# First modulation in four steps of 256 channels, idle matmuls during the input loads, tiles 4 to 7 in buffers of their own, sines at a fixed place

## Chip, cores and metric

The kernel runs on one core of a Trainium2 chip. The metric is device time in microseconds: the median of the runs shown. A core has TensorE (PE, the matrix engine, with weight loads shown apart as PEld), VectorE (DVE), ScalarE (ACT), GpSimd (POOL) and SyncE (SP, which here only issues DMAs). Each engine works through a queue of its own in order; semaphores tie the queues together.

## What is computed

Two layers of a hybrid decoder block over 1024 tokens of width 1024, all in fp32. The part that matters here is the head of a layer:

```python
mod = c_act @ w_mod + b_mod
shift, scale, gate = jnp.split(mod[:, None, :], 3, axis=-1)
h = rms_norm(x, pre_gain) * (1.0 + scale) + shift
proj = h @ w_in
(aq, ak, av, ag, rq, rk, rv, rg, gq, gk, gv, gg, ga) = jnp.split(proj, IN_SPLITS, axis=-1)
```

`c_act = silu(c)` is one vector of 1024. Three groups of heads follow (windowed attention and retention with rotary angles from `positions`, and gated linear attention), then gates, an output projection and `x + gate * rms_norm(y)`.

## The kernel before

A token tile is 128 tokens; tiles 0 to 3 are handled by `first_stage`, tiles 4 to 7 by jobs that run behind it. A projection is done with fp32r operands split in a high and a low part (`hi`, `lo`), three passes: hi by hi, hi by lo, lo by hi. `hT[(0, p)]` holds the transposed, modulated input of two tiles, in both parts. `gg`, `rg`, `rq`, `rk` are blocks of 256 columns of `w_in`; `gg` carries 16 extra columns for the gate logits, hence 272. A block is loaded in four DMAs into `st` buffers (five of them) and converted by ACT (high part, L495) and POOL or DVE (low part, L499).

What `first_stage` does (L674 to L804), in its order:

- Loads: ACT issues the identity, the positions, the bias rows (L679, L680), the frequencies of the rotary tables (`freq`) and `w_ga`. SP issues the four x tiles, then the first layer's shift and scale weights `wm` (8 MB, eight blocks of 128 channels, two DMAs each, L694) with the four `gg` loads between them, then the four `rg` loads.
- `tables` (L360) computes the rotary angles on DVE: about 15 operations of 128x512, which the caller takes one at a time with `more(n)`. Near its end ACT computes two sines (L385, L386), each with a table of its own function to be loaded; tanh is in another table.
- For each x tile: the sum of squares on ACT (L727), one step on DVE (L604), a power on POOL (L607), the scaling on DVE (L732).
- Eight steps, one per block `b` of 128 channels. `turn(b)` transposes the four tiles' block into two PSUM tiles `at` (pool `mm`, three banks) and multiplies `c_act` by `wm` into `pm`: eight matmuls of 256 columns, four at a time in column groups. Then ACT copies the row out (L761), two matmuls with the vector `sel` bring it into columns ("selections"), DVE makes `gain` and `shift` (L767, L769), and the transposed tiles are scaled and shifted: tiles 0 and 1 on ACT (L777, high part L778), tiles 2 and 3 on DVE (L774, L775), the low parts on DVE (L779). `products(b - 1, ...)` multiplies the block before by `gg`, 12 matmuls of 272 columns in the accumulators `acc[0..3]`; they stand around the selections, so that PE has work while the others make the columns.

After that the four `rg` conversions, the products of the last block, and the loads of tiles 4 to 7: into the two halves of a buffer of tag `mx` (L794), into `kT0`, and into two `t2` buffers (L798). These buffers held x tiles 0 to 3 before. Then the projection of `rg` begins (79 matmuls of 256 columns in a row), in which the jobs for tiles 4 to 7 are mixed: squares on ACT (L621), scaling on DVE (L637), for each tile two groups of four transposes (L187, pool `aux`, five banks), read by ACT (L651) and DVE (L653), conversions L657 and L658.

Outside `first_stage` a planner with a clock of its own (`clk`, the costs in the table `L`) decides where in PE's order a job's matmuls stand; the other engines' order is then set by a scheduler. Inside it the order is that of the code. The end of the sines and the transposes of their table are such a job (`table_job`).

Of the kernel before, what the change touches and what calls it, by code (L numbers as in the profile page):

```python
# [17 lines left out]
P = 128  # L18
# [75 lines left out]
def trunk(ctx: ExitStack, tc: tile.TileContext, ins, cst, out):  # L94
# [579 lines left out]
    def first_stage():  # L674
        for j in range(2):
            mod_tile(0, j)
        shift, gain = modc[(0, 0)], modc[(0, 1)]
        rows = t1()[0:24, 0:P]
# [4 lines left out]
        freq = cload("freq", eng=A)  # L683
# [5 lines left out]
        wm = bp.tile([P, 4 * SLOT], F32, tag="arena1", name="wm").rearrange("p (b k n) -> p b k n", b=KT, k=KT)  # L689
        gg, rg = load(0, "gg", "AG"), load(0, "rg", "AV")  # L690
        gg.issue()
        def wm_load(b):
            for i in range(2):
                nc.sync.dma_start(wm[:, b, 4 * i:4 * i + 4], w_m0[b, :, 4 * i:4 * i + 4].rearrange("p k j n -> p k (j n)"))  # L694

        for b in range(KT - 1):
            wm_load(b)
            if b in (1, 3, 4):
                gg.issue()
# [9 lines left out]
        pposf = aux()  # L709
        transp(pposf[:, 0:8], posr, ident[0:8, 0:8])  # L710
        V.tensor_copy(posf, pposf[:, 0:8])
        more(1)
# [3 lines left out]
        more(2)  # L716
        pr = aux()
        transp(pr[:, 0:24], rows, ident[0:24, 0:24])
        rc = small(24)
        V.tensor_copy(rc, pr[:, 0:24])  # L720
        base = small(8)
        V.tensor_scalar(base, rc[:, 8:16], 1.0, None, ALU.add)
        sel = small(1)
        V.tensor_reduce(sel, ident[:, 0:97:32], AX.X, ALU.add)
        for t in range(4):
            ss = small(1)
            A.activation(wm[:, KT - 1, 4 * (t % 2):4 * (t % 2) + 4].rearrange("p k n -> p (k n)"), xe[t], AF.Square, accum_out=ss)  # L727
            r = rstd_of(ss, 1, 1.0 / D, EPS)
            if t == 3:
                A.activation(w[:, 0, :, 256:272], low, AF.Copy)  # L730
                V.tensor_tensor(w[:, 1, :, 256:272], low, f(w[:, 0, :, 256:272]), ALU.subtract)
            V.tensor_scalar(xe[t], xe[t], r, None, ALU.mult)  # L732
        gg.convert()
        wm_load(KT - 1)
        for _ in range(4):
            rg.issue()
        acc = [aux() for _ in range(4)]
        pm = aux()
# [3 lines left out]
        def products(b, ts):  # L742
            for t in ts:
                h = hT[(0, t // 2)]
                c = slice((t % 2) * P, (t % 2) * P + P)
                for i, (x, y) in enumerate(((0, 0), (0, 1), (1, 0))):
                    mult(acc[t][:, 0:272], h[:, x, b, c], w[:, y, b, 0:272], b == 0 and i == 0, b == KT - 1 and i == 2)

        def turn(b):
# [9 lines left out]
        for b in range(KT):  # L759
            row = t1()  # L760
            A.activation(row, pm[:, 0:256], AF.Copy)  # L761
            if b:
                products(b - 1, (0,))
            c0 = 256 + 2 * b
            for j in range(2):
                mult(pm[:, c0 + j:c0 + j + 1], row[:, j * P:(j + 1) * P], sel, True, True)
            V.scalar_tensor_tensor(gain[:, b:b + 1], pm[:, c0 + 1:c0 + 2], base[:, b:b + 1], rc[:, 16 + b:17 + b],  # L767
                                   ALU.add, ALU.mult)
            V.tensor_tensor(shift[:, b:b + 1], pm[:, c0:c0 + 1], rc[:, b:b + 1], ALU.add)  # L769
            for p in range(2):  # L770
                hf = t1()
                hi, lo = (hT[(0, p)][:, a, b, 0:256] for a in range(2))
                if p:
                    V.tensor_scalar(hf, at[p][:, 0:256], gain[:, b:b + 1], shift[:, b:b + 1], ALU.mult, ALU.add)  # L774
                    V.tensor_copy(hi, hf)  # L775
                else:
                    A.activation(hf, at[p][:, 0:256], AF.Identity, scale=gain[:, b:b + 1], bias=shift[:, b:b + 1])  # L777
                    A.activation(hi, hf, AF.Copy)  # L778
                V.tensor_tensor(lo, hf, f(hi), ALU.subtract)  # L779
            if b:  # L780
                products(b - 1, (1, 2, 3))
            if b < KT - 1:
                at = turn(b + 1)
            if b in (0, 2, 4):
                gg.convert()
            if b < 6:
# [4 lines left out]
        products(KT - 1, range(4))  # L791
        x6 = gp.tile([P, D], F32, tag="kT0", name=nm("xk"), bufs=1)
        for t, xt in zip(range(4, NT), x_pair() + [x6]):
            nc.sync.dma_start(xt, x_in[0, t * P:(t + 1) * P, :])  # L794
            late.append([xt[:, 512 * j:512 * j + 512] for j in range(2)])
        late.append([t2(), t2()])
        for j in range(2):
            nc.sync.dma_start(late[3][j], x_in[0, 7 * P:8 * P, 512 * j:512 * j + 512])  # L798
# [4 lines left out]
        late.append(sin)  # L803
# [41 lines left out]

# [970 lines left out]
```

## Time and profile before

| | us |
|---|---|
| median of 3 runs | 994.59 (992.64 to 995.18) |
| profiled execution | 999.38 |
| its span, first to last instruction | 997.7 |
| PE busy in it | 963.3 (97%) |
| granted PE clock, mean | 0.992 |

A row of the timeline has start, duration, engine, line, operation, out<-in with the shape, and the number of instructions merged; in brackets the idle time ahead of it and what ended that. `SPq` and `ACTq` are the queues that issue DMAs. In a row of the windows `(x25)` is a number of instructions, and the number behind the five engines is the granted PE clock as a share of full speed. One fp32 matmul shows as two matmul records.

### The profile page before, as it was taken

Reading aid. Unit: us, or ns where it says so; the run is one execution under the profiler, and the core shown is the slowest. Engines: PE = TensorE matmul, PEld = TensorE weight load, DVE = VectorE, ACT = ScalarE, POOL = GpSimd, SP = SyncE. Lnnn points to the kernel's source line nnn. Section 1 sums busy time; section 2 is a strip of 40 time slices with the busy share of each in tenths; the row PEclk is TensorE's granted clock in tenths of the full one; section 3 lists DMA queues with packets and bytes.
Section 4 is the critical chain, followed back from the end, with each engine's and each line's share of the span. In section 5 each row is a group of like instructions: output and inputs, shape, how many; then the busy total and the mean of one; then the engine's idle time right before and its main releaser. Section 6 shows DMA issues by size and latency. Waiting matters only on the chain. (4 is left out here: it accounts for less than half of the span.)

```text
span 997.7 us, 19627 instructions
## 1 busy us (share of the span) xinstructions
PE 963.3 (97%) x7188; PEld 826.3 (83%) x7188; DVE 681.6 (68%) x1622; ACT 400.8 (40%) x1127; POOL 246.6 (25%) x310
## 2 busy tenths in 40 slices
PE   3979999999999999999999999999999999999996
PEld 1779999989997777777879999998999877777775
DVE  3668667867666787665598176785766577676876
ACT  3387210333322565633356232133332256664231
POOL 2132101233220233430115010123322033544000
PEclk9998999999999999999999999999999999999998
DMA  9456713433225355577656131242122324388783
GB/s 344 170 163 182 206 60 106 152 109 104 93 91 185 90 148 160 179 230 250 216 202 210 48 107 33 93 151 85 50 97 86 127 76 134 112 271 262 247 274 125
DMA packets 109457, 150.35 MB, mean 151 GB/s; under 512 B 12168, under 2 KB 59820, under 8 KB 109360
## 3 DMA queue, kind: packets, MB, share of 16 engines
q1 hardware_dynamic: 97920, 134.75, 43.0%
q10 hardware_dynamic: 11440, 14.34, 3.9%
q8 instruction: 57, 0.93, 0.4%
q14 instruction: 40, 0.33, 0.1%
HBM read 110.25 MB, written 36.70 MB: 147 GB/s over the span
## 5 line engine op out<-in xcount | busy, mean ns | idle before, releaser
L172 PE MATMUL mm<-arena,arena 128*128 128x256 f32 (+2 forms) x1824 | 300.5, 318 | 0.5 <-DVE t L1233 0.4
L172 PE MATMUL mm<-arena 128*128 128x256 f32 (+2 forms) x1728 | 284.9, 318 | 0.0
L172 PEld LDWEIGHTS mm<-arena,arena 128*128 128x128 f32 x1824 | 255.3, 191 | 26.0 <-issue 4.8
L172 PEld LDWEIGHTS mm<-arena 128*128 128x128 f32 x1728 | 240.4, 189 | 24.3 <-issue 4.2
L172 PE MATMUL mm<-arena,mx 128*128 128x512 f32 (+1 forms) x564 | 130.9, 388 | 0.5 <-DVE t L1434 0.5
L607 POOL TENSOR_TENSOR sm<-sm,mhalf 128x1 f32<-128x1 f32 (+1 forms) x64 | 56.8, 888 | 297.5 <-DVE sm L604 162.5
L172 PEld LDWEIGHTS mm<-arena,mx 128*128 128x128 f32 x564 | 101.5, 188 | 24.6 <-issue 1.5
L156 ACT ACTIVATE t<-aux 128x256 f32<-128x256 f32 (+2 forms) x124 | 52.3, 437 | 93.5 <-PE aux L187 80.0
L156 ACT ACTIVATE arena<-st 128x512 fp32r<-128x512 f32 x94 | 56.1, 628 | 48.3 <-DMA st<-in_w_in_dram 17.1
L499 POOL TENSOR_TENSOR arena<-st,arena 128x512 fp32r<-128x512 f32 x31 | 45.0, 1451 | 116.1 <-ACT arena L156 74.9
L991 POOL TENSOR_TENSOR smx<-smx,sm 128x512 f32<-128x512 f32 x32 | 35.0, 1094 | 134.2 <-DVE sm L990 113.2
L987 ACT ACTIVATE smx<-smx,sm 128x129 f32<-128x129 f32 x128 | 49.9, 393 | 32.7 <-DVE sm L984 32.6
L499 DVE TENSOR_TENSOR arena<-st,arena 128x512 fp32r<-128x512 f32 x77 | 59.9, 799 | 4.1 <-ACT arena L156 2.4
L318 DVE SCALAR_TENSOR_TENSOR acc<-ms,c_act,acc 128x512 f32<-128x512 f32 x60 | 45.1, 751 | 15.3 <-DMA ms<-in_w_mod_dram 14.7
L1035 ACT ACTIVATE t<-aux 128x256 f32<-128x256 f32 x32 | 12.3, 384 | 77.5 <-PE aux L172 71.3
L172 PEld LDWEIGHTS aux<-t,mx 32*128 32x128 f32 (+1 forms) x896 | 39.8, 187 | 3.9 <-issue 1.7
L172 PE MATMUL aux<-t,mx 32*128 32x32 f32 (+1 forms) x896 | 40.9, 272 | 0.0
L187 PE MATMUL aux<-c_ident,t 128*128 128x128 f32 (+2 forms) x187 | 33.2, 277 | 5.2 <-DMA t<-in_pre_norm_gain_dram 3.3
L1337 DVE SCALAR_TENSOR_TENSOR t<-t,sm,t 128x512 f32<-128x512 f32 x32 | 23.3, 752 | 20.2 <-DMA t<-in_x_dram 13.5
L982 DVE COPY_PREDICATED smx<-c_curmask,aux 128x256 f32<-128x256 int32 x64 | 25.3, 446 | 16.4 <-ACT smx L156 14.6
L172 PEld LDWEIGHTS aux<-kT,mx 64*128 64x128 f32 x384 | 24.7, 185 | 11.8 <-issue 5.2
L1040 DVE TENSOR_TENSOR t<-aux,sm 128x256 f32<-128x256 f32 x32 | 13.6, 425 | 27.3 <-POOL sm L607 27.3
(252 smaller groups left out, 1435.1 us busy)
## 6 DMA issues: line engine op xcount, KB each, us to landing
st<-in_w_in_dram SPq DMA_DIRECT2D x96, 256.0 KB, 4.0
ms<-in_w_mod_dram SPq DMA_DIRECT2D x64, 256.0 KB, 3.7
mx<-mixS SPq DMA_DIRECT2D x20, 512.0 KB, 5.2
st<-in_w_last_dram SPq DMA_DIRECT2D x36, 256.0 KB, 3.7
wm<-in_w_m_dram SPq DMA_DIRECT2D x16, 512.0 KB, 9.7
mixS<-t SPq DMA_DIRECT2D x40, 128.0 KB, 1.9
t<-in_x_dram SPq DMA_DIRECT2D x18, 256.0 KB, 6.1
mixS<-t ACTq DMA_DIRECT2D x32, 128.0 KB, 3.1
```

Of the source, the lines that this page charges most:

```text
L156: A.activation(dst, src, AF.Copy)
L172: T.matmul(dst, lhsT, rhs, start=start, stop=stop)
L187: T.transpose(dst, src, idn)
L318: V.scalar_tensor_tensor(acc, wt, c_act[:, k:k + 1], acc, ALU.mult, ALU.add)
L499: e.tensor_tensor(lo, st, f(hi), ALU.subtract)
L607: G.tensor_tensor(r, r, mhalf[:, :w], ALU.pow)
L982: V.copy_predicated(sv, curmask.unsqueeze(1).to_broadcast((P, 2, P)), pv[:, :, n // P - 1, :])
L987: A.activation(sm[:, h, :], sm[:, h, :], AF.Exp, bias=mx[:, h:h + 1], accum_out=sums[:, h:h + 1])
L991: eng("pn").tensor_tensor(sm[:, :, 0:128], sm[:, :, 0:128], rs.unsqueeze(2).to_broadcast((P, 4, P)), ALU.mult)
L1035: A.activation(sq, po, AF.Square)
L1040: V.tensor_tensor(h4(g1), h4(po), r.unsqueeze(2).to_broadcast((P, 4, 64)), ALU.mult)
L1337: V.scalar_tensor_tensor(xt[j], yg[j], r, xt[j], ALU.mult, ALU.add)
```

## The change

- `wm` is cut in four steps of 256 channels. A step does eight transposes, eight matmuls of 512 columns into all of `pm`, four selections, and scales and shifts both of its blocks: the first on ACT, the second on DVE, each for all four tiles at once (512 columns). The selections write to a bank `pc` of the pool `mm`, which it keeps for the whole stage. The products of a step (24 matmuls) follow one step later; for step 1 three tiles of them stand ahead of the selections, otherwise one; after the last step they run pass by pass over all tiles.
- `spin(n)` multiplies the identity by itself into an accumulator that is overwritten later: 6 times after the transpose of the positions, 18 times after that of the bias rows, 6 times in step 1.
- The frequencies are loaded ahead of the bias rows. All angle operations on DVE now have fixed places (three ahead of the tiles, one with each of tiles 0 to 2, eight after step 0's `turn`), the two sines stand after step 0 on ACT, one table load for both, and a tanh of no use to the result after step 2 brings tanh's table back. `table_job` is gone; the table's transposes are a job of their own, due after 16.0 instead of the old delays.
- Tiles 4 to 7 are loaded in halves into three `smx` buffers, three of the modulation's buffers (`ms`) and the two `t2` buffers.

```diff
-        for b in range(KT - 1):
-            wm_load(b)
-            if b in (1, 3, 4):
-                gg.issue()
+        for s in range(3):
+            gg.issue()
+            wm_load(s)
+        acc = [aux() for _ in range(4)]
+        pm = aux()
+        def spin(n):
+            for _ in range(n):
+                mult(acc[3][:, 0:P], ident, ident, True, True)
...
         def turn(b):
-            for t in range(4):
-                transp(at[t // 2][:, t % 2 * P:t % 2 * P + P], xe[t][:, b * P:b * P + P], ident)
+            for i in range(2):
+                for t in range(4):
+                    transp(at[i][:, t * P:t * P + P], xe[t][:, (2 * s + i) * P:(2 * s + i + 1) * P], ident)
+            if s == 1:
+                spin(6)
             for k in range(KT):
                 g = k % 4
-                mult(pm[32 * g:32 * g + 32, 0:256], c_act[:, k:k + 1].to_broadcast((P, 32)), wm[:, b, k], k < 4, k > 3, 0.11)
+                mult(pm[32 * g:32 * g + 32, :], c_act[:, k:k + 1].to_broadcast((P, 32)), wm[:, s, k], k < 4, k > 3, 0.22)
...
         at = turn(0)
-        for b in range(KT):
+        more(8)
+        for s in range(4):
+            row = t2()
+            A.activation(row, pm, AF.Copy)
+            n = 3 if s == 1 else 1
+            if s:
+                products(s - 1, range(n))
+            for i in range(4):
+                mult(pc[:, 4 * s + i:4 * s + i + 1], row[:, i * P:(i + 1) * P], sel, True, True)
...
+            if s < 3:
+                at = turn(s + 1)
+                gg.convert()
+            if s == 0:
+                more(1)
+            elif s == 1:
+                more(2)
+            elif s == 2:
+                A.activation(th0, c_nat, AF.Tanh, scale=0.5)
...
-        x6 = gp.tile([P, D], F32, tag="kT0", name=nm("xk"), bufs=1)
-        for t, xt in zip(range(4, NT), x_pair() + [x6]):
-            nc.sync.dma_start(xt, x_in[0, t * P:(t + 1) * P, :])
+        kept = [gp.tile([P, 528], F32, tag="smx", name=nm("xl"), bufs=SMB)[:, 0:512] for _ in range(3)]
+        kept += [mod_stage() for _ in range(3)] + [t2(), t2()]
+        for t in range(4, NT):
+            xt = kept[2 * t - 8:2 * t - 6]
+            for j in range(2):
+                nc.sync.dma_start(xt[j], x_in[0, t * P:(t + 1) * P, 512 * j:512 * j + 512])
```

PE's order at the start of the program, before (`c_ident` is the identity, `xk` and `mx` are x tiles 0, 1 and 2, 3, `arena` holds weights and `hT`):

```order
L187 MATMUL aux_137<-c_ident,posr 128x8
L187 MATMUL aux_147<-c_ident,t_6_98 128x24
L187 MATMUL mm_198<-c_ident,xk_105 128x128
L187 MATMUL mm_198<-c_ident,xk_106 128x128
L187 MATMUL mm_199<-c_ident,mx_107 128x128 x2
L172 MATMUL aux_197<-wm,c_act 32x256 x8
L172 MATMUL aux_197<-sm_153,t_40_212 128x1 x2
```

and now:

```order
L187 MATMUL mm_132<-c_ident,posr 128x8
L172 MATMUL aux_128<-c_ident 128x128 x6
L187 MATMUL mm_148<-c_ident,t_6_100 128x24
L172 MATMUL aux_128<-c_ident 128x128 x18
L187 MATMUL mm_218<-c_ident,xk_105 128x128
L187 MATMUL mm_218<-c_ident,xk_106 128x128
L187 MATMUL mm_218<-c_ident,mx_107 128x128 x2
L187 MATMUL mm_219<-c_ident,xk_105 128x128
L187 MATMUL mm_219<-c_ident,xk_106 128x128
L187 MATMUL mm_219<-c_ident,mx_107 128x128 x2
L172 MATMUL aux_129<-wm,c_act 32x512 x8
L172 MATMUL mm_217<-sm_170,t_41_244 128x1 x4
```

Twenty-four idle matmuls stand ahead of the first tile, and a step has twice the transposes and selections.

ACT's order from the last block's scaling (L777) to the squares of tile 4 (L621), before (`sm` and `t` are small tiles and tiles of 256 or 512 columns):

```order
L777 ACTIVATE t_76_501<-mm_478,mod_4_96,mod_5_97 128x256
L385 ACT_TABLE_LOAD
L385 ACTIVATE sincos<-mx_140 128x8x64
L778 ACTIVATE arena_71<-t_76_501 128x256
L495 ACTIVATE arena_518<-st_185 128x512
L495 ACTIVATE arena_518<-st_187 128x512
L495 ACTIVATE arena_518<-st_189 128x512
L495 ACTIVATE arena_518<-st_191 128x512
L1060 ACTIVATE sm_586<-aux_193 128x16
L1052 ACT_TABLE_LOAD
L1052 ACTIVATE t_86_591<-aux_193 128x256
L1060 ACTIVATE sm_596<-aux_194 128x16
```

and now, from the last step's scaling (L802):

```order
L802 ACTIVATE t_61_433<-mm_396,mod_4_96,mod_5_97 128x512
L803 ACTIVATE arena_71<-t_61_433 128x2x256
L495 ACTIVATE arena_459<-st_209 128x512
L495 ACTIVATE arena_459<-st_211 128x512
L495 ACTIVATE arena_459<-st_213 128x512
L495 ACTIVATE arena_459<-st_215 128x512
L1087 ACTIVATE sm_546<-aux_125 128x16
L1079 ACTIVATE t_75_551<-aux_125 128x256
L1087 ACTIVATE sm_556<-aux_126 128x16
L1079 ACTIVATE t_79_561<-aux_126 128x256
```

The sine and the table loads are gone from this place; the second sine (L386), which stood a few rows further with two more table loads around it, is gone from there too.

SP's order behind the last gg load, before (`st` are weight blocks):

```order
L694 DMA wm<-in_w_m_dram 128x1024 x6
L161 DMA st_185<-in_w_in_dram 128x512
L161 DMA st_187<-in_w_in_dram 128x512
L161 DMA st_189<-in_w_in_dram 128x512
L161 DMA st_191<-in_w_in_dram 128x512
L794 DMA mx_540<-in_x_dram 128x1024 x2
L794 DMA xk_539<-in_x_dram 128x1024
L798 DMA t_80_544<-in_x_dram 128x512
L798 DMA t_81_545<-in_x_dram 128x512
```

and now:

```order
L694 DMA wm<-in_w_m_dram 128x2048 x2
L161 DMA st_209<-in_w_in_dram 128x512
L161 DMA st_211<-in_w_in_dram 128x512
L161 DMA st_213<-in_w_in_dram 128x512
L161 DMA st_215<-in_w_in_dram 128x512
L831 DMA xl_492<-in_x_dram 128x512
L831 DMA xl_493<-in_x_dram 128x512
L831 DMA xl_494<-in_x_dram 128x512
L831 DMA ms_495<-in_x_dram 128x512
```

The place in the queue is the same; the buffers written are others, and each tile comes in two halves.

More of the change, by code (lines that the diff above doesn't have):

```diff
@@ L733, in first_stage, with product, products @@
         gg.convert()
-        wm_load(KT - 1)
+        gg.issue()
+        wm_load(3)
         for _ in range(4):
             rg.issue()
-        acc = [aux() for _ in range(4)]
-        pm = aux()
         for p in range(2):
             hT[(0, p)] = place(TOK[0][p])
-        def products(b, ts):
+        def product(t, b, x, y, start, stop):
+            h = hT[(0, t // 2)]
+            mult(acc[t][:, 0:272], h[:, x, b, (t % 2) * P:(t % 2) * P + P], w[:, y, b, 0:272], start, stop)
+        def products(s, ts):
@@ L802, in first_stage @@
             flag(("hT", 0, t))
-        late.append(sin)
         return acc
@@ L1757, in trunk @@
     job(gla_log(0, 0))
-    job(table_job(late[4]))
+    job(tables_T())
     job(late_consts())
```

112 lines of the change are left out of this document (54 added, 58 removed).

## Prediction

> **What bounds the kernel now.** I read the page's busy times first, then busy time by stage, then by shorter stretches for the granted clock, then the timeline of the stages that have holes.
>
> ```profile
> span 997.7 us, 19627 instructions
> ...
> PE 963.3 (97%) x7188; PEld 826.3 (83%) x7188; DVE 681.6 (68%) x1622; ACT 400.8 (40%) x1127; POOL 246.6 (25%) x310
> ```
>
> TensorE (PE) is busy 97% of the span, so 34.4 us of holes are all that any change to waits can win, plus what PE loses while its clock is granted at half. The busy times by stage (columns: length, busy time of PE, weight loads, DVE, ACT, POOL, granted clock, DMA share, GB/s) show where the holes are:
>
> ```profile
> 0.00:30.00 30.00, 13.83 (x74) 8.51 (x78) 12.65 (x34) 10.06 (x19) 6.38 (x16) 1.00 0.94 354
> 52.78:58.33 5.55, 2.81 (x13) 2.22 (x13) 3.57 (x8) 5.52 (x9) 1.17 (x1) 0.91 0.90 305
> 71.70:100.00 28.30, 25.20 (x187) 24.84 (x185) 23.27 (x58) 21.13 (x52) 6.86 (x9) 0.88 0.63 186
> 100.00:980.00 880.00, 875.52 (x6558) 752.40 (x6557) 607.64 (x1438) 341.98 (x992) 219.90 (x264) 1.00 0.46 144
> ```
>
> From 100 to 980 us PE has 4.5 us of holes; before 100 us it has 16.2 + 2.7 + 3.1 = 22 us, all where the change works. A hole costs twice, as the next table shows, cut at multiples of 3.41 us:
>
> ```profile
> 23.17:26.59 3.42, 3.42 (x25) 2.38 (x18) 2.52 (x6) 0.38 (x1) 1.11 (x1) 1.00 1.03 395
> 26.59:30.00 3.41, 3.41 (x21) 2.71 (x23) 2.21 (x6) 0.98 (x2) 0.00 (x0) 1.00 1.02 414
> 50.46:53.87 3.41, 2.32 (x16) 1.95 (x16) 2.02 (x7) 2.05 (x3) 0.00 (x0) 1.00 0.93 332
> 53.87:57.28 3.41, 1.76 (x9) 1.17 (x9) 2.52 (x7) 3.38 (x9) 0.12 (x1) 1.00 1.00 340
> 57.28:60.70 3.42, 3.42 (x17) 3.42 (x17) 3.19 (x4) 3.38 (x5) 3.29 (x5) 0.50 0.24 43
> 70.93:74.34 3.41, 1.37 (x13) 1.07 (x11) 2.49 (x8) 3.41 (x11) 0.00 (x0) 1.00 0.74 200
> 74.34:77.76 3.42, 2.36 (x11) 2.36 (x12) 2.67 (x8) 2.67 (x10) 1.73 (x2) 0.50 0.55 147
> 77.76:81.18 3.42, 3.42 (x17) 3.42 (x16) 2.11 (x5) 1.42 (x3) 0.62 (x1) 0.50 0.76 170
> ```
>
> After a window in which PE was busy 1.76 or 1.37 of 3.41 us the clock is half for at least the next window; 2.32 us kept it; a half-clock window of 2.36 us did not bring it back, one of 3.42 us did. So a window of 3.41 us decides, somewhere between 1.8 and 2.3 us of work to keep the clock, and above 2.4 us to regain it. The Trainium skill (TensorE: Matmul & The Clock Gate, Part 1: The HAM clock gate) says the same of a free-running window of 3413 ns with two rates; the trace agrees, as all four edges lie whole windows apart.
>
> In the first 30 us the clock column shows 1.00 only because no change of it had been recorded yet. The durations show half pace:
>
> ```profile
> 17.52 1.94 PE L172 MATMUL aux<-wm,c_act 128*32 128x256 f32 x16
> 26.06 2.39 PE L172 MATMUL aux<-arena 128*128 128x272 f32 x9
> 33.37 1.07 PE L172 MATMUL aux<-wm,c_act 128*32 128x256 f32 x16
> 34.95 0.60 PE L172 MATMUL aux<-sm,t 128*128 128x1 f32 x4
> 35.42 1.38 PE L172 MATMUL aux<-arena 128*128 128x272 f32 x9
> 36.64 0.38 PE L187 MATMUL mm<-c_ident,xk 128*128 128x128 f32 x2
> ```
>
> The same 16 passes take 1.94 us early and 1.07 us later, nine products 2.39 and 1.38 us; counted in windows back from 57.28, full pace begins at 30.0. So PE is late in the first stage because it waits for the inputs, and then works 12 us at half pace.
>
> **The change, part by part.** First the inputs:
>
> ```profile
> 6.78 0.27 PE L187 MATMUL aux<-c_ident,t 24*128 24x24 f32 x1 [3.25 <-DMA t<-in_pre_norm_gain_dram]
> 8.03 0.69 DVE L364 TENSOR_TENSOR mx<-sm,c_freq 128x512 f32<-128x512 f32 x1 [4.30 <-DMA c_freq<-cst_freq_dram]
> 13.84 0.75 DVE L732 TENSOR_SCALAR mx<-mx,sm 128x1024 f32<-128x1024 f32 x1 [0.66 <-POOL sm L607]
> 15.32 1.74 DVE L732 TENSOR_SCALAR mx<-mx,sm 128x1024 f32<-128x1024 f32 x1 [0.46 <-POOL sm L607]
> ...
> 48.02 1.41 DVE L379 SCALAR_TENSOR_TENSOR mx<-mx 128x512 f32<-128x512 f32 x2
> ```
>
> The DVE queue stands until the frequencies land at 8.03; the two loads ahead of them landed by 6.78. The change issues the frequencies first: they land by 6.8 (bounds: 5.1 to 8.03, with the bias rows then at up to 8). DVE then does three sine steps of at most 0.70 us (1.41 for two) and c_act, about 2 us. A tile takes 1.48 us now (13.84 to 15.32): 0.75 of scaling and 0.73 of a round trip to POOL, into which one sine step just fits. I take 1.6 a tile, and 0.5 more at tile 1, where the bias steps now stand. The first scaling so starts at 9.5 and the last, at 1.74 us as now, ends at about 16.5, against 15.32 + 1.74 = 17.06 (bounds 15.5 and 17.7).
>
> The idle matmuls. One fp32 matmul shows as two records (8 in the program, 16 in the trace). The nearest dense records are the 256-column ones, which occupy PE as long as 128 fp32 columns would:
>
> ```profile
> 58.33 10.57 PE L172 MATMUL mm<-arena,arena 128*128 128x256 f32 x79
> 68.73 1.03 PE L187 MATMUL aux<-c_ident,mx 128*128 128x128 f32 x8
> 69.53 1.90 PE L172 MATMUL mm<-arena,arena 128*128 128x256 f32 x14
> 75.40 1.11 PE L187 MATMUL aux<-c_ident,mx 128*128 128x128 f32 x4 [3.10 <-ACT t L651]
> 76.17 4.16 PE L172 MATMUL mm<-arena,arena 128*128 128x256 f32 x17
> ```
>
> 17 take 3.96 us from start to start at half clock, 0.233 each; the first 79 took 10.40, of which 2.37 us at half clock hold 10, so the other 69 took 0.117 each. An idle matmul thus costs 0.47 or 0.23 us (bounds: 0.22 at full pace from the transposes, 8 in 1.03 us; twice 0.47 if its two weight loads do not overlap). Six fill 3.5 to 6.3 us, where PE idles anyway. Eighteen start at about 7.5 and run at half pace until a window has been full, 10.9 to 14.3 by phase; in the middle they end at 14.2, ahead of the last tile, so they cost nothing. Did they never speed up, they would end at 16.0, still not late; at the upper price, and never sped up, they would end near 24 and cost 8 us.
>
> Step 0 from 16.5: five transposes to 17.2; eight 512-column modulation matmuls at twice 1.07 us to 19.3. Their 2.1 MB follow the four x tiles (2.1 MB) and one weight block, 4.6 MB with the small loads. By 30 us 10.6 MB have moved (354 GB/s), the last of it at 414 GB/s, so 4.6 MB are reached 14.5 us earlier, at 15.5: just hidden. The rest needs these rows:
>
> ```profile
> 30.71 0.39 ACT L761 ACTIVATE t<-aux 128x256 f32<-128x256 f32 x1 [3.07 <-DMA wm<-in_w_m_dram]
> 52.19 0.56 ACT L777 ACTIVATE t<-mm,mod,mod 128x256 f32<-128x256 f32 x1 [1.35 <-DVE mod L769]
> 52.77 1.28 ACT L385 ACT_TABLE_LOAD   x1
> 54.60 0.40 ACT L778 ACTIVATE arena<-t 128x256 fp32r<-128x256 f32 x1
> 55.05 0.52 PE L172 MATMUL aux<-arena 128*128 128x272 f32 x2 [2.27 <-ACT arena L778]
> 92.07 0.60 ACT L401 ACTIVATE t<-aux 128x512 f32<-128x512 f32 x1 [1.08 <-PE aux L187]
> ```
>
> A 512-column copy takes 0.60 where 256 take 0.39; by the same ratio the 512-column scaling is 0.85. So: row copy to 20.0, four selections (0.47 a pair, 34.95 to 35.42) to 20.95, three small DVE operations to 21.5, scaling to 22.4. The eight sine steps now queued ahead of these on DVE last at most 5.6 us from 16.5: they are done before 22.1, so they cost between nothing and 1 us; I take nothing, since three of them are plain TENSOR_SCALARs. Only now may the transposes of step 1 start, since the column tile keeps one of the three mm banks. Then 8 transposes, 6 idle matmuls, 8 modulation matmuls: 0.9 + 1.4 + 2.1 at full pace, 1.6 + 2.8 + 3.9 at half. Between 14.2 and 22.4 the only dense work is 2 us, so I expect the clock to fall within step 0 and to return when the second idle matmuls have filled a window. The end of step 1's modulation is then about 29.5; 26.8 if full pace is never lost; 33.4 if it is already gone at 16.5 (step 0 alone then takes 2.7 us more).
>
> What remains to the first rg matmul, now at 58.33: 96 products at 0.136 (35.42 to 36.64) 13.1, twelve selections 2.85, 16 transposes 1.8, 16 modulation matmuls 4.2, and one wait of 0.5 after step 1's selections, where only six products cover DVE and ACT: 22.4. Before, two channel blocks needed the same work, so the four-step form itself gains nothing here. The sines go: ACT's table load at 52.77 stood between scaling and conversion of the last block, and PE waited 2.27 us; both loads now run after step 0, under 4 to 8 us of PE work, and the return to tanh under step 2's products. What is late next is DVE's last subtraction, about 3 us after step 3's selections; 34 products (4.6 us) come first, so nothing waits. The rg matmuls start at 51.9 (49.2 to 55.8): **6.4 us gained** (2.5 to 9.1).
>
> Without the hole no half-clock window falls on the rg matmuls: 2.37 us at half pace did 1.2 us of work, **1.2 gained**.
>
> Tiles 4 to 7. Today their loads wait for the x buffers (issue at 49.42); in buffers of their own they follow the last rg load.
>
> ```profile
> 35.13 0.33 SPq L161 DMA_DIRECT2D st<-in_w_in_dram  x1
> 49.42 0.80 SPq L794 DMA_DIRECT2D mx<-in_x_dram  x2
> 70.19 1.50 ACT L651 ACTIVATE t<-aux,mod,mod 128x128 f32<-128x128 f32 x4
> 73.83 1.52 ACT L651 ACTIVATE t<-aux,mod,mod 128x128 f32<-128x128 f32 x4
> ```
>
> So they land some 10 us earlier, and four table loads leave ACT's queue. Yet the 3.10 us wait at 75.40 is not for data: the eighth transpose group in a rotation of five aux banks waits until ACT has read the third, and ACT does squares and conversions between 70.19 and 75.35. That order is unchanged. Only the delay from 68.73 to 70.19 can shrink, from 1.46 to the 0.5 us of the transposes: **0.9 gained**, 2.2 us of wait remain. These still spoil a window in most phases. Today 5.8 us from 75.40 to 81.18 run at half pace, 2.9 lost; one window of 3.41 costs 1.7: **1.2 gained** (0 to 2.9).
>
> Sum: 6.4 + 1.2 + 0.9 + 1.2 = 9.7 us. The profiled execution took 999.38 us (span 997.7), so 989.7 for it; it lies 4.8 us above the median of the runs, 994.59, from which the forecast is 984.9.
>
> **Rivals.** *The clock is lost before step 0.* After the idle matmuls PE holds only transposes until 17.2. If these count as idleness, the window to about 17 has at most 1 us of work, and step 0 runs at half pace: rg at 55.8, sum 2.5 + 1.2 + 0.9 + 1.2 = 5.8, **988.8**. The Trainium skill speaks for this (same page, Part 4: PE-mode transpose): transposes do not count as PE-busy. Against it: the window 26.59:30.00, which brought the clock back, held about 0.8 us of transposes, with 2.6 us of other work. Chance 0.24.
>
> *No window is lost at all,* neither in step 0 nor at the aux wait: 9.1 + 1.2 + 0.9 + 2.9 = 14.1, **980.5**. Against it speak 1.76 and 1.37. Chance 0.12.
>
> *Slower: the mm bank that the column tile holds.* In steps 1 to 3 PE cannot start the next transposes until both halves are scaled. I hide this under 18 products (2.45 us). If DVE is slowed as at 15.32 (1.74 for 0.75), PE waits 1.4 us per step, and a window that falls under 1.8 us of work costs 1.7 more, two per step if it does not refill: 3 x (1.4 + 3.4) = 14.4, giving 994.59 - 9.7 + 14.4 = **999.3**. It decides from 9.7 us on, some two waits with two lost windows each. Against it: the change leaves more products behind each selection than now. Chance 0.06.
>
> *Given back.* The loads and DVE work after 100 us are reordered (table stores now ahead of some weight loads); with 4.5 us of holes in 880 the stretch is tight, and a weight 9 us late would eat it all: **994**. Chance 0.05.
>
> **How the numbers follow.** The forecast has 0.53, with 981.5 to 988 as its own range. 984.9 is the likeliest case. The range 980 to 991 takes in the first two rivals and leaves out the last two and the far end of the first. A run tells 0.3%, 3 us, from no change. Faster: 0.53 + 0.12 + 0.21 of the 0.24 = 0.86; same: 0.05 + 0.03 = 0.08; slower 0.06.
>
> **What would show it.** In the changed profile: 18 idle matmuls, their pace doubling before 14.3; the last scaling done near 16.5; step 1's modulation ending at 28 to 32; no sine load between scaling and conversion at the end; rg at 49 to 55; a wait of about 2 us before tile 5's second transposes. Wrong would be: rg after 57, a wait in every step, or new holes after 100 us.

## The result, and the profile after

The changed kernel takes 987.13 us (median of five runs, 985.62 to 988.55) against 994.59 (five runs, 992.64 to 996.36): a ratio of 0.9929, 95% interval 0.9909 to 0.9949. It was timed a second time beside the kernel before: 986.08 against 995.26, ratio 0.9904 (0.9887 to 0.9922). So it is 7.5 to 9.2 us faster; 9.7 were forecast. The profiled execution took 987.97 us.

The page of the changed kernel, span and busy times:

```profile
span 986.0 us, 19571 instructions
...
PE 963.0 (98%) x7184; PEld 830.4 (84%) x7184; DVE 682.5 (69%) x1602; ACT 396.2 (40%) x1114; POOL 246.2 (25%) x310
```

PE is busy as long as before; its idle time is 23.0 us instead of 34.4. That is no measure of the gain: the 30 idle matmuls count as busy, some 12 us here, and no_idle below, which leaves them out, has 31.0 us of idle PE (985.5 less 954.5) in the same time. Two stretches of the changed kernel (columns as in the prediction; `rg` starts at 52.11):

```profile
46.76:52.11 5.35, 5.35 (x45) 5.35 (x44) 5.03 (x10) 4.04 (x10) 1.10 (x1) 1.00 0.30 74
...
100.00:970.00 870.00, 867.37 (x6487) 744.50 (x6486) 611.25 (x1431) 340.07 (x986) 219.40 (x262) 1.00 0.46 146
```

The stretch ahead of `rg`, 2.81 us of work in 5.55 before, has no hole left, and `rg` starts at full clock. PE's timeline of the first stage:

```profile
8.14 6.34 PE L172 MATMUL aux<-c_ident 128*128 128x128 f32 x36
...
17.66 0.33 PE L187 MATMUL mm<-c_ident,mx 128*128 128x128 f32 x1 [2.21 <-DVE mx L745]
...
18.36 1.92 PE L172 MATMUL aux<-wm,c_act 128*32 128x512 f32 x16
21.00 1.05 PE L172 MATMUL mm<-sm,t 128*128 128x1 f32 x8 [0.72 <-ACT t L782]
23.69 0.69 PE L187 MATMUL mm<-c_ident,xk 128*128 128x128 f32 x2 [1.65 <-ACT t L802]
...
25.46 2.76 PE L172 MATMUL aux<-c_ident 128*128 128x128 f32 x12
28.15 2.59 PE L172 MATMUL aux<-wm,c_act 128*32 128x512 f32 x16
30.67 2.52 PE L172 MATMUL aux<-arena 128*128 128x272 f32 x18
...
35.31 0.44 PE L187 MATMUL mm<-c_ident,xk 128*128 128x128 f32 x2 [0.46 <-ACT t L802]
...
46.76 5.51 PE L172 MATMUL aux<-arena 128*128 128x272 f32 x42
52.11 8.13 PE L172 MATMUL mm<-arena,arena 128*128 128x256 f32 x67
...
67.33 1.11 PE L187 MATMUL aux<-c_ident,ms 128*128 128x128 f32 x4 [2.27 <-ACT t L651]
```

The idle matmuls run from 8.14 and are done at 14.3. Step 0's modulation runs at full pace (1.92 us). Then PE waits for the row copy and for the scaling, loses the clock at 22.7, and the six idle matmuls and half of step 1's modulation run at half pace (granted clock 0.50 from 22.72 to 29.55). From 35.31 on a step takes 6.93 us, and `rg` starts 6.2 us earlier than at 58.33. The wait at tile 5 is 2.27 us, where it was 3.10. ACT at the end of the stage:

```profile
47.40 0.78 ACT L802 ACTIVATE t<-mm,mod,mod 128x512 f32<-128x512 f32 x1 [1.61 <-DVE mod L792]
48.21 0.63 ACT L803 ACTIVATE arena<-t 128x512 fp32r<-128x512 f32 x1
```

Nothing stands between scaling and conversion now, and PE's 42 records at 46.76 cover both.

### The profile page after: what moved, and what is told of

It reads as the page before. It is cut to its first block, busy times and chain, and to the rows that moved or that the text cites. A ratio compares the mean times of both kernels' runs of the same rounds, so it can differ in the third digit from the quotient of the medians.

```text
span 986.0 us, 19571 instructions
## 1 busy us (share of the span) xinstructions
PE 963.0 (98%) x7184; PEld 830.4 (84%) x7184; DVE 682.5 (69%) x1602; ACT 396.2 (40%) x1114; POOL 246.2 (25%) x310
## 3 DMA queue, kind: packets, MB, share of 16 engines
q10 hardware_dynamic: 11440, 14.34, 4.0%
## 5 line engine op out<-in xcount | busy, mean ns | idle before, releaser
L187 PE MATMUL aux<-c_ident,t 128*128 128x128 f32 x186 | 32.9, 277 | 1.5 <-ACT t L1194 0.9
```

The source lines that it names most:

```text
L187: T.transpose(dst, src, idn)
```

## The experiments

The theory at the start: the gain comes from earlier inputs, from a clock that the idle matmuls hold and from the sines' new place, and the four-step form and the buffers are worth nothing by themselves. The rival: the idle matmuls are neutral, and the form carries the gain. Each kernel ran in five rounds beside the kernel before; `rg` and the idle time of PE are from its one profile. Kernels that were not timed side by side are compared by their ratios.

| kernel | us (lowest to highest) | ratio to before, interval | rg | PE idle, 100 to 970 |
|---|---|---|---|---|
| changed | 987.13 (985.62 to 988.55) | 0.9929, 0.9909 to 0.9949 | 52.11 | 2.6 |
| no_idle | 987.03 (984.04 to 987.75) | 0.9911, 0.9894 to 0.9928 | 50.29 | 3.7 |
| sines_late | 988.42 (986.8 to 989.0) | 0.9927, 0.9912 to 0.9943 | 52.63 | 2.8 |
| old_x | 987.55 (985.9 to 991.28) | 0.9924, 0.9905 to 0.9943 | 51.28 | 3.2 |
| eight_steps | 991.6 (990.76 to 994.37) | 0.9968, 0.9952 to 0.9983 | 56.83 | 3.9 |
| front_idle | 988.6 (985.15 to 989.17) | 0.9919, 0.99 to 0.9938 | 49.95 | 5.1 |
| bridge | 984.71 (981.84 to 986.15) | 0.9885, 0.9867 to 0.9903 | 47.31 | 3.4 |
| aux_idle | 986.18 (984.81 to 987.6) | 0.9905, 0.9889 to 0.9921 | 51.09 | 2.4 |
| eight_spread | 996.85 (994.7 to 998.87) | 1.0015, 1.0002 to 1.0028 | 57.29 | 4.3 |
| four_alone | 991.65 (990.61 to 992.13) | 0.9961, 0.9944 to 0.9977 | 55.80 | 3.0 |
| bridge_aux | 982.15 (981.29 to 983.5) | 0.9864, 0.9845 to 0.9884 | 47.44 | 3.3 |
| after_again | 986.08 (984.4 to 987.82) | 0.9904, 0.9887 to 0.9922 | 51.82 | 2.2 |
| before_again | 995.42 (993.22 to 998.61) | 1.0, 0.9987 to 1.0014 | 57.41 | 3.4 |

**no_idle**: the changed kernel without any idle matmul.

```diff
-            for _ in range(n):
+            for _ in range(0):
                 mult(acc[3][:, 0:P], ident, ident, True, True)
```

> The changed kernel without its 30 idle matmuls, all else the same. Theory (the idle matmuls gain because PE reaches full pace earlier): PE runs at half pace from the first transposes until about 31 to 33 us, step 0 takes some 2.7 us more, step 1 saves the 2.8 us of its idle matmuls; the rg matmuls start at 53.5 to 54.5 instead of 52.1, and the time is 1.5 to 2.5 us above the changed kernel, so 5 to 6 us below the kernel before. Rival (the clock is lost in step 0 anyway, so the idle matmuls are worth nothing): the rg matmuls start at 51.5 to 52.5 and the time is that of the changed kernel, 7.5 us below the kernel before.

It is as fast as the changed kernel. PE's timeline:

```profile
17.84 3.43 PE L172 MATMUL aux<-wm,c_act 128*32 128x512 f32 x16
...
26.27 2.63 PE L172 MATMUL aux<-wm,c_act 128*32 128x512 f32 x16
```

Step 0's modulation is 1.5 us longer at half pace (3.43 for 1.92), but the 2.7 us of the six idle matmuls at 25.46 are gone; with step 0's modulation starting 0.5 us sooner in this execution (17.84 for 18.36), `rg` stands 1.8 us earlier. That is earlier than both expectations had it. The theory is wrong here and the rival right in the time: in this pair of profiles 30 idle matmuls win 1.5 us and cost 2.7.

**front_idle**: the changed kernel without the six in step 1.

```diff
-            if s == 1:
-                spin(6)
```

> The changed kernel without the six idle matmuls of step 1; the first 24 stay. Theory (the first 24 buy full pace for step 0's modulation, worth about 1.5 us on PE's path; the six stand at half pace between step 1's transposes and its modulation and cost the 2.7 us that they last): rg matmuls start at 50 to 50.7, 1 to 2 us below the changed kernel, so 8.5 to 9.5 us below the kernel before on this chip. Rival (idle matmuls are worth nothing anywhere, because the clock's fixed windows give back what they take): rg at 51.5 to 52.5, the time of the changed kernel within 1 us.

Step 0's modulation in PE's timeline, and the late stretch by the windows:

```profile
17.45 3.48 PE L172 MATMUL aux<-wm,c_act 128*32 128x512 f32 x16
```

```profile
100.00:970.00 870.00, 864.90 (x6468) 742.08 (x6467) 611.87 (x1430) 338.92 (x982) 216.66 (x262) 1.00 0.46 145
```

`rg` starts 2.2 us earlier (49.95), a little ahead of what the theory expected, but not for its reason: the first 24 idle matmuls did not buy full pace, step 0's modulation took 3.48 us behind them. The 2.2 us are the 2.7 of the six, 1.0 of inputs that came sooner in this execution (the last scaling released PE at 16.67 for 17.66), less the 1.5 of the half pace. In the time nothing is won: 988.6, a ratio between the changed kernel's two. This execution has 5.1 us of idle PE behind 100 us, 2.5 more than the changed kernel's. Over the fourteen profiles this figure lies between 2.2 and 5.1 without an order that follows `rg`, so whether the 2 us are given back as a rule or only by chance is open.

**sines_late**: the changed kernel with the first sine between the last step's scaling and conversion, the second behind the `rg` conversions, and no tanh ahead of them; the angle operations stay early.

```diff
+                    if s == 3:
+                        more(1)
                     A.activation(hi, hv, AF.Copy)
...
-            if s == 0:
-                more(1)
-            elif s == 1:
-                more(2)
-            elif s == 2:
-                A.activation(th0, c_nat, AF.Tanh, scale=0.5)
```

> The changed kernel with its two sines put back: the first between scaling and conversion of the last step, the second behind the rg conversions. Theory (the sine's table load in that place made PE wait and lose the clock): conversion of the last step comes 1.9 us later, PE waits 1.5 to 2 us ahead of the last products, one window at half clock follows (1.7 us), and ACT is late for tile 5 by some of its two more table loads: 3 to 5 us above the changed kernel. Rival (the hole at the end of the first stage came from something else): no new wait ahead of the last products, within 1 us of the changed kernel.

PE's timeline:

```profile
29.49 2.54 PE L172 MATMUL aux<-arena 128*128 128x272 f32 x18
...
49.52 3.27 PE L172 MATMUL aux<-arena 128*128 128x272 f32 x24 [1.42 <-ACT arena L806]
```

The hole is back, shorter than the 2.27 us of before since 18 products stand ahead of it. From the end of step 1's modulation to `rg` it is 23.14 us (29.49 to 52.63) where the changed kernel has 21.44, and 21.46 in its second profile (30.36 to 51.82): 1.7 us for the sines. In the time it is less than the theory's 3 to 5 and not settled: the ratio is that of the changed kernel's first timing (0.9927 and 0.9929) and 2.3 us above that of its second (0.9904).

**old_x**: the changed kernel with tiles 4 to 7 in the buffers of before.

```diff
-        kept = [gp.tile([P, 528], F32, tag="smx", name=nm("xl"), bufs=SMB)[:, 0:512] for _ in range(3)]
+        x6 = gp.tile([P, D], F32, tag="kT0", name=nm("xk"), bufs=1)
+        for t, xt in zip(range(4, NT), x_pair() + [x6]):
```

> The changed kernel with tiles 4 to 7 loaded into the buffers that they had before. Theory (the wait ahead of tile 5's second transposes is ACT's queue, not data): the loads start at about 43 us when the buffers come free and land by 50, before ACT wants them at 52; the wait stays 2.2 to 2.5 us and the time is within 0.7 us of the changed kernel. Rival (the early loads gain): squares wait for loads, tile 5's wait grows to 3 us or more, 2 us or more above the changed kernel.

PE's second transposes of tile 5:

```profile
66.50 0.66 PE L187 MATMUL aux<-c_ident,mx 128*128 128x128 f32 x4 [2.29 <-ACT t L651]
```

Same time, and the same shortened wait at tile 5 (2.29 us): the buffers are worth nothing, and the wait shrank for another reason.

**eight_steps**: all of the change except the form; the modulation in eight steps of 128 channels, with the eight angle operations behind the first `turn` (a part of its edit against the kernel before).

```diff
+            if b == 1:
+                spin(6)
...
         at = turn(0)
+        more(8)
         for b in range(KT):
```

> The kernel before with everything of the change but the four steps: eight steps of 128 channels, the 30 idle matmuls (the last six in the second step), the frequencies first, the sines after the second step, tiles 4 to 7 in buffers of their own. Theory (the four-step form gains nothing): within 1 us of the changed kernel, rg matmuls at 51 to 53. Rival (the four steps carry the gain): rg matmuls after 55 and 3 us or more above the changed kernel.

PE's transposes of the second block:

```profile
22.31 0.69 PE L187 MATMUL mm<-c_ident,mx 128*128 128x128 f32 x2 [2.96 <-ACT t L792]
```

It gains 4.2 us where the changed kernel gains 7.5 to 9.2. But the first step of 128 ends at 19, and DVE's eight operations hold its columns until 21.4: 2.96 us of wait that the form alone does not explain. So the next kernel spread them.

**eight_spread**: eight_steps with its angle operations in pairs, behind the first `turn` and behind each of steps 0 to 2, and the sines behind step 3 (the edit is against eight_steps).

```diff
-        more(8)
+        more(2)
...
-            if b == 1:
-                more(1)
+            if b < 3:
+                more(2)
```

> As eight_steps (the first modulation in eight steps of 128 channels, all else as changed), but the eight angle operations are spread, two behind each of the steps 0 to 3, and the sines stand behind step 3. Theory (four steps of 256 gain nothing over eight of 128; eight_steps lost its 4 us because DVE's eight angle operations stood ahead of a first step that ends earlier): rg at 52 to 53.5, within 1 us of the changed kernel, 6.5 to 8 us below the kernel before. Rival (the four-step form itself carries the gain, since each step's chain of copy, selections, columns and scaling is paid half as often): rg at 55 or later, 3 us or more above the changed kernel.

PE's timeline, the longest of its waits (ahead of selections):

```profile
40.00 0.61 PE L172 MATMUL aux<-sm,t 128*128 128x1 f32 x4 [1.17 <-ACT t L776]
```

It is as slow as the kernel before, and the theory that the form gains nothing falls. A step of 128 channels takes 3.8 us where nothing waits (27.72 to 31.51), two of them 7.6 where a step of 256 takes 6.9; with angle operations on DVE or the sines on ACT in it, the chain of copy, selections, columns and scaling takes longer, and PE waits 0.2 to 1.2 us at four places. A further 2.0 us wait, on a weight conversion on DVE after 100 us, and a half-clock window behind it (113.87 to 117.28) belong to this kernel's order and not to the question; by an estimate from these rows they are some 3.7 us of its time (2.0 and half of 3.41), and without them it would still stand well above the changed kernel.

**four_alone**: the kernel before with nothing but the form.

```diff
-        for b in range(KT):
-            row = t1()
+        for s in range(4):
+            row = t2()
...
-            if b < 6:
-                more(1)
+            if s < 3:
+                more(2)
```

> The kernel before with nothing but the first modulation in four steps of 256 channels: no idle matmuls, the frequencies behind the bias rows, sines, angle operations and x buffers as before. Theory (the four-step form carries the gain by itself: a step of 256 channels takes 6.9 us where two of 128 took 8, and leaving out the idle matmuls, the early sines or the buffers cost 0, 1.3 and 0 us): rg matmuls start at 53 to 55, the time 5 to 7 us below the kernel before, 1 to 2 us above the changed kernel. Rival (the parts work only together; the two eight-step kernels lost to the angle operations in DVE's queue, not to their form): rg at 56 to 58, within 3 us of the kernel before.

PE's timeline, and ACT's first sine:

```profile
34.17 0.44 PE L187 MATMUL mm<-c_ident,xk 128*128 128x128 f32 x2 [0.47 <-ACT t L787]
...
41.10 0.38 PE L187 MATMUL mm<-c_ident,xk 128*128 128x128 f32 x2
...
50.26 0.39 PE L172 MATMUL aux<-arena 128*128 128x272 f32 x1 [2.12 <-ACT arena L788]
51.41 4.60 PE L172 MATMUL aux<-arena 128*128 128x272 f32 x23 [0.75 <-DVE arena L785]
55.80 9.65 PE L172 MATMUL mm<-arena,arena 128*128 128x256 f32 x79
...
71.14 0.66 PE L187 MATMUL aux<-c_ident,mx 128*128 128x128 f32 x4 [2.29 <-ACT t L651]
...
47.73 0.63 ACT L385 ACTIVATE sincos<-mx 128x512 f32<-128x512 f32 x1 [1.77 <-DVE mx L381]
```

Between the two expectations: 3.6 us below the kernel before, `rg` at 55.80. The step is the fast one (6.93 us from 34.17 to 41.10), but the sines still stand at the end (2.12 and 0.75 us of wait), and the window behind that hole runs at half clock: 23 records take 4.39 us to `rg`, where the changed kernel's 42 take 5.35. Without both, `rg` would come at some 51.0 (an estimate: 45.63, where the 18 products ahead of the hole begin, and the changed kernel's 5.35 us for 42 in a row). The hole is not the sines' alone: both stand ahead of the last scaling here, and the first waits 1.77 us for DVE's last angle operation (L381). So the form carries a part of the gain, and the early place of sines and angle operations another; the angle operations' place was not tried by itself. The wait at tile 5 is 2.29 us here too, in the old buffers: what shrank it is not the buffers.

**bridge**: the changed kernel with the idle matmuls where PE stands idle in the first steps, none in step 1.

```diff
+                    if s == 0 and i == 0 and t == 3:
+                        spin(8)
...
-            if s == 1:
-                spin(6)
...
+            else:
+                spin(3)
...
+            else:
+                spin(7)
```

> The changed kernel with the idle matmuls of step 1 moved to where PE stands idle: eight more between the third and the fourth tile's first transposes, three ahead of step 0's selections, seven behind them. Theory (what is left to win in the first stage is the clock that is lost at 22.7 and comes back at 29.5): the clock is held from about 14 us on, step 1's modulation ends at 27, rg at 48 to 49, 3 to 4 us below the changed kernel, some 11 below the kernel before. Rival (DVE's eight angle operations, done at 22.4, and the copy, column and scaling steps bound the stage, so that PE's pace is covered): rg at 50.5 to 51.5, 1 to 1.5 us below the changed kernel.

PE's timeline: the last idle matmuls and step 1's modulation:

```profile
21.21 1.81 PE L172 MATMUL aux<-c_ident 128*128 128x128 f32 x14
...
24.02 1.92 PE L172 MATMUL aux<-wm,c_act 128*32 128x512 f32 x16
```

The clock, full from 11.9 us on, is not lost ahead of `rg`, which starts at 47.31, 4.8 us earlier than in the changed kernel. In the stage the theory is right, and the rival (DVE bounds the stage) is not. In the time the gain is less sure than its 3 to 4 us: 4.4 by the ratio of the changed kernel's first timing, 1.9 by that of its second, whose interval overlaps bridge's; this profile loses a window behind tile 5's wait (63.06 to 66.47), the second one of the changed kernel does not.

**aux_idle**: the changed kernel with eight idle matmuls ahead of tile 5's second transposes.

```diff
+            if (l, t, j) == (0, 5, 1):
+                idle = mm()
+                for _ in range(8):
+                    mult(idle[:, 0:P], ident, ident, True, True, 0.0)
```

> The changed kernel with eight idle matmuls into a free bank ahead of tile 5's second transposes, where PE waits 2.3 us for ACT. Theory (the half-clock window behind that wait is lost because the window ahead holds under 2 us of work): the wait is filled, no half clock after it, 0.5 to 1.7 us below the changed kernel. Rival (the idle matmuls outlast the wait, or the phase of the windows spares it anyway): from the same to 0.4 us above the changed kernel.

PE's timeline behind the idle matmuls:

```profile
66.32 0.65 PE L187 MATMUL aux<-c_ident,ms 128*128 128x128 f32 x4 [0.50 <-ACT t L655]
66.73 2.36 PE L172 MATMUL mm<-arena,arena 128*128 128x256 f32 x17
```

The wait is filled but for 0.50 us, the 17 records behind it take 2.36 us where the first profile of the changed kernel had 3.44, and the ratio is 0.9905. That is what the theory expected, but the second timing of the changed kernel (0.9904) is as good: by the time alone it is not settled.

**bridge_aux**: both.

> The idle matmuls of bridge and of aux_idle together in the changed kernel. Theory (the two win in different places, the clock in steps 0 and 1 and the window behind the aux wait): rg at 47 to 48, no half clock from 14 us to the end, 3 to 4 us below the changed kernel, 10.5 to 12 us below the kernel before. Rival (what is won ahead of 100 us is partly given back in short waits behind it, as in front_idle, where rg stood 2.2 us earlier and the time did not): no more than 2.5 us below the changed kernel, with 4 us or more of idle PE between 100 and 970.

982.15 us, 3.9 below the changed kernel timed beside it (after_again): the theory's 3 to 4, and the fastest version here. Its profile records no half clock until the last 5.3 us of the program (974.75), where the other profiles have it too; the window behind tile 5's second transposes (62.67):

```profile
62.40:65.80 3.40, 3.13 (x26) 3.13 (x27) 3.34 (x8) 2.79 (x9) 0.00 (x0) 1.00 0.58 133
```

**after_again** and **before_again**: the two kernels, profiled a second time.

> The changed kernel once more, beside the others on one chip, with a second profile. If the profiled execution was a usual one: rg at 51.5 to 52.5, the idle of PE from 100 to 970 between 2 and 4 us, 987 us in the runs. If the phase of the clock's windows moves from run to run: one window more or fewer than the first profile's three at half pace, with rg up to 1.7 us off.

> The kernel before once more with a second profile. Theory (the first profile, 999.38 us, overstated the lost clock by its phase and held more short waits than usual): a time of 993 to 996, with less than 5.8 us at half clock behind the aux wait or in the rg matmuls. Rival (profiled executions of this kernel are always slower by that much): 998 to 1000 again, with the same half-clock windows.

The kernel before, second profile:

```profile
57.41 10.24 PE L172 MATMUL mm<-arena,arena 128*128 128x256 f32 x79
67.49 1.04 PE L187 MATMUL aux<-c_ident,mx 128*128 128x128 f32 x8
...
74.49 0.66 PE L187 MATMUL aux<-c_ident,mx 128*128 128x128 f32 x4 [3.17 <-ACT t L651]
74.90 2.35 PE L172 MATMUL mm<-arena,arena 128*128 128x256 f32 x17
```

The changed kernel, second profile:

```profile
17.81 3.58 PE L172 MATMUL aux<-wm,c_act 128*32 128x512 f32 x16
...
28.50 1.92 PE L172 MATMUL aux<-wm,c_act 128*32 128x512 f32 x16
...
51.82 9.54 PE L172 MATMUL mm<-arena,arena 128*128 128x256 f32 x79
61.20 1.03 PE L187 MATMUL aux<-c_ident,xl 128*128 128x128 f32 x8
...
67.05 0.66 PE L187 MATMUL aux<-c_ident,ms 128*128 128x128 f32 x4 [2.29 <-ACT t L651]
```

These executions took 994.51 and 985.84 us. The first profile of the kernel before was an unlucky one: it had 5.8 us at half clock behind the wait at tile 5, this one has none (17 records in 2.35 us). And the changed kernel can lose the clock elsewhere without loss: here step 0's modulation runs at half pace (3.58 us), step 1's at full pace (1.92), and `rg` starts at 51.82 all the same.

## Why the prediction was right, and where it was not

The sign, the size within 0.5 to 2.2 us, the start of `rg` (51.9 forecast, 52.11 and 51.82 measured) and the range were right. Between the second profiles (8.7 us) the sum is: `rg` earlier by 5.6 (57.41 to 51.82); 0.7 less from there to tile 4's transposes (10.08 and 9.38 us); 1.15 less from there to the end of the wait at tile 5 (7.00 and 5.85 us); 1.1 less idle PE from 100 to 970 us (3.4 and 2.2). That is 8.5. Term by term:

- **rg earlier, 6.4 forecast: 6.2 and 5.6.** Right as a sum, wrong in its parts, and near by luck: step 1's modulation ended 1.2 us late (30.67 for 29.5), and the rest took 21.4 us where 22.4 were added up. The step that failed is "Before, two channel blocks needed the same work, so the four-step form itself gains nothing here". The inputs won next to nothing: the last scaling released PE at 17.66, a microsecond behind the 16.5 that was forecast, where before's did at 17.11. Over all profiles DVE gets the frequencies at 6.7 to 7.8 us in the new order and at 7.9 to 8.0 in the old, but from there to this release it needs 9.9 us instead of 9.1, with angle operations now between the tiles. The release came at 16.9 on the mean, instead of 17.0. And DVE's eight angle operations, put at nothing, held step 0's columns until 22.41, some 0.3 us behind the end of the selections (21.00 and 1.05). Two steps of the kernel before, first profile, run from the first of these rows to the second:

```profile
32.84 0.38 PE L187 MATMUL mm<-c_ident,xk 128*128 128x128 f32 x2
...
40.78 0.38 PE L187 MATMUL mm<-c_ident,xk 128*128 128x128 f32 x2
```

  The fourth block's modulation ends there at 34.4 (33.37 and 1.07). At the like point, 30.67 (forecast 29.5), the changed kernel still owes 24 products and two selections that are done in the other: at 0.127 (42 in 5.35 us) and 0.47 a pair some 3.5 us, so it stands at 34.2 and has won next to nothing. All of the gain comes behind this point. From 34.4 to 52.78 the kernel before needs 18.4 us for what takes the changed one 16.4 (34.2 to 52.11 without the last 12 products at 1.5): 2.0 for the form, since two blocks took 7.94 us (32.84 to 40.78), a step takes 6.93, and two are left. Of the 1.0 a step, 0.4 is in the products (3.57 us for 24 in rows of 3 and 9, 3.20 in rows of 6 and 18), 0.4 in the transposes with the small waits ahead of them, the rest in modulation and selections. Then come the 5.55 us from 52.78 to 58.33, in which the last 12 products stood: 4.0 for the sines' hole, 2.74 of it waits (2.27, 0.24 and 0.23, as the sums of one profile), the rest the products' three short bursts. Together 6.0. That the form has a part is what eight_spread and four_alone show. That the sines have one is shown in the stage by sines_late, 1.7 us; how the 4.0 divide among sines, angle operations and the rows of products that now cover them is not shown.
- **Idle matmuls, cost nothing.** Right for the first 24 (done at 14.3; 14.2 forecast). But they do not hold the clock: of the six profiles that have these 24 alone ahead of a four-step form, three have step 0's modulation at full pace (the first one, sines_late, aux_idle), and three at half pace for most or all of it (3.58 us in the second one, 3.48 in front_idle, 3.18 in old_x). The six at half pace cost 2.7 us on PE's path, which the forecast had counted (2.8) without asking whether leaving them out is better. no_idle shows that it is no worse.
- **rg at full clock, 1.2.** Right in kind, by phase in size: 1.0 against the first profile (10.40 and 9.37 us from `rg` to tile 4's transposes), 0.7 against the second.
- **The wait at tile 5, 0.9.** 0.8 in the first profiles, right in size. Half of the reason fell: in old_x and four_alone the tiles lie in the old buffers and the wait is 2.29. What these kernels share with the changed one is that ACT has fewer table loads in that stretch: none in the changed kernel and one in four_alone, where before had three between 57 and 62 us. Just ahead of that read ACT stood 2.47 us in the kernel before, waiting for DVE (L1054) and not for a table, so the loads do not delay it directly. That they are the cause was not tried by itself.
- **The half clock behind that wait, 1.2.** This term stands on one execution. Of the twelve profiles with this wait unfilled, five lost nothing there (both second ones among them), six lost one window and one, the first, lost two. It is no property of either kernel, and the forecast should have taken a mean over phases for both.
- **The base.** Setting the sum of 9.7, worked out against an execution of 999.38, against the median of 994.59 counted that execution's bad phase as gain. The first profiles differ by 11.7 us of span, the second by 8.9, the medians by 7.5 and 9.2.

The rival *the clock is lost before step 0* came true in the second profile (and in front_idle's and old_x's) and did not cost its 3.9 us. Its windows:

```profile
14.34:17.75 3.41, 0.97 (x6) 0.67 (x6) 2.84 (x6) 0.00 (x0) 1.78 (x2) 1.00 1.02 425
17.75:21.16 3.41, 3.41 (x18) 0.59 (x16) 3.24 (x6) 0.00 (x0) 0.00 (x0) 0.51 0.99 414
21.16:24.57 3.41, 1.35 (x13) 1.04 (x10) 2.01 (x7) 1.47 (x3) 0.00 (x0) 0.99 1.04 438
24.57:27.98 3.41, 3.41 (x17) 3.41 (x18) 1.66 (x3) 3.38 (x5) 1.69 (x1) 0.51 1.02 423
```

A lost window full of work brings the clock back at its end; a window with 1.35 us of work loses it again, and that second loss is over before step 1's modulation. The forecast had added a loss in step 0 to the whole loss in step 1. Here two windows are lost whichever come, in all eight profiles that have the 24 idle matmuls and not bridge's; no_idle runs as much of these steps at half pace (step 0's modulation to 20.92, then from 24.34 to 27.75). Only filling the holes, as bridge does, saves both. The mm bank, as a wait in every step, did not come: PE waits 0.46 us once behind step 1's selections, where 0.5 was forecast. Nor did late weights eat the gain.

## What to carry to other kernels

Split a stage at the last point where both kernels have done the same work, and see which side of it the gain lies on: here the inputs, which got most of the attention, gave next to nothing, and the later steps' pace and the hole at the stage's end gave all. A term that rests on a half-clock window in one profile is a matter of phase: price it over several executions, for both kernels. Idle matmuls pay where they fill every hole until the work is dense (bridge_aux, 3.9 us); a few of them, or some that stand in PE's way at half pace, give back what they win.

## What the runs showed of the clock

The prediction put the work that keeps the clock between 1.8 and 2.3 us of a window. The first profile of the changed kernel does not fit that:

```profile
15.90:19.31 3.41, 1.65 (x17) 0.89 (x21) 3.31 (x5) 0.00 (x0) 1.16 (x1) 1.00 0.98 399
19.31:22.72 3.41, 2.02 (x20) 1.03 (x12) 3.24 (x8) 0.60 (x1) 0.00 (x0) 1.00 1.01 421
22.72:26.13 3.41, 2.44 (x12) 2.44 (x13) 2.64 (x6) 3.21 (x4) 1.23 (x1) 0.50 1.00 423
```

1.65 us kept the clock and 2.02 lost it, though 1.05 of the 2.02 are the selections of one column. Busy time alone does not decide; that one-column matmuls count for less would fit, but no run tried it. The Trainium skill (TensorE: Matmul & The Clock Gate, Part 4: PE-mode transpose) says that transposes do not count as busy in the same way. The 0.97 us that lost the clock at 14.34 in the second profile are all transposes, which would fit. But the window of 1.65 holds some 0.7 us of them and kept the clock with 0.95 us of other work, while the one of 2.02, with 0.97 us beside its selections, lost it. Neither reading is shown. At half clock, 2.44 us of work did not bring the full clock back.
